# Hybrid decoder, two layers: the pre-norm weight folded into the splitting of the projection weights, and the order of the first tiles and of the layer's end written out

## The chip, the cores and the metric

The kernel runs on one core of a Trainium2 chip. The metric is device time in microseconds (us) of one execution. A core has five engines that each run their own queue of instructions in order: PE (matmul), ACT, DVE and POOL (elementwise work), and SP, which here only issues DMAs.

## The reference

Two layers work on 512 tokens of width 1024. Cut to what matters here:

```python
def rms_norm(x, g):
    return x * lax.rsqrt(mean(x * x, axis=-1) + 1e-6) * g

def hybrid_layer(x, w_in, w_out, g_pre, g_post, ...):
    h = rms_norm(x, g_pre)
    proj = einsum('bsd,de->bse', h, w_in)      # 1024 -> 6400 columns
    ... HGRN2 recurrence (8 heads), sliding-window attention (16 heads), gates ...
    y = einsum('bse,ed->bsd', concat([o_h, o_a]), w_out)   # 2048 -> 1024
    return x + rms_norm(y, g_post)
```

The weight `g_pre` of the first norm scales the columns of `h`, which are the rows of `w_in`: scaling `h` by it or scaling the rows of `w_in` gives the same product.

## The kernel before, in words

**Products in three passes.** Every projection is computed in a reduced float format with both operands split in a high and a low half; `mm3` (L174 to L177) adds stationary high times moving low (or the reverse), low times high, and high times high. So each operand has to be split first. Activations are split when they leave PSUM: `split_psum` (L266 to L268) copies the high half on ACT (`hhi`) and subtracts on DVE (`hlo`). Weights are split by `w_conv`: a piece of 128x512 comes by DMA into one of three `raw` buffers (`w_load`, L152), ACT copies the high half (`whi`, L169), and DVE or POOL subtracts it to get the low half (`wlo`, L170). A raw buffer is free for the next DMA only when the low half of the piece in it is done. There are 264 pieces: per layer 4 for keys and values (`wkv`, two row blocks of 256 columns each), 96 of `w_in` in twelve slabs of eight, and 32 of `w_out`. POOL takes every second piece of `wkv` and of the first slab `QA`, 12 pieces in all; DVE does the other 252.

**Order of the work.** `step()` emits one k step of a projection at a time (three matmuls), then runs what was put off with `later(steps, key, fn)` and is due, then calls `w_conv` so that conversion stays `LEAD` = 4 pieces ahead. `ensure` runs what is still put off when a unit needs its key. Instructions are ordered on each engine by a scheduler that goes by the order in which the program emits them and by its estimate of when their operands are ready; `pin` puts an instruction behind the instruction of the same engine that was emitted just before it. SP issues its DMAs in order too, so a DMA that waits for a buffer holds up those behind it.

**Pre-norm.** `pre_norm` does one tile of 128 tokens: two squares with row sums on ACT (L302, into the one buffer `u`), a sum on DVE (L280), the power -1/2 on POOL (L282), two multiplications by that and by `g_pre` on DVE (L306, `xn`), four transposes on PE for each half (L311), and the split (L267 and L268). Before the first layer it is emitted for all four tiles, ahead of everything else. `g_pre` is read as a row copied to all 128 partitions, two DMAs of 256 KB in each layer (L292).

**End of a layer.** The last output projection (`out` `h1`) runs token tile by token tile. For each half the result is added on DVE (`y`, L732) and squared on ACT (L758); POOL multiplies the first half by `g_post` (L760), DVE the second (L763); then rstd, two fused multiply-adds on DVE (L766) and the DMAs to memory (L767). In layer 0 the next layer's `pre_norm` of the same tile follows at once, and its transposes and splits are put off by `DEFER` = 18 steps. The key and value projection of layer 1 needs them first (`PE pj L175` on `wkv`), then slab `QA`.

## Time and profile before

| | us |
|---|---|
| median of 3 runs (972.87 to 973.04) | 973.0 |
| profiled execution, own time | 975.33 |
| its span | 973.5 |
| PE busy | 921.1 |
| DVE busy | 739.5 |
| ACT busy | 446.6 |
| POOL busy | 289.2 |
| mean granted clock of PE | 0.983 |

The profile is one execution of its own. Its time lies 2.3 us above the median, and 1.8 us of its time lie outside the span. PE is busy for 95% of the span, so the time is that of PE plus the stretches in which PE waits or runs at a lower clock.

### The profile page before, as it was taken

The page shows a single profiled execution, that of the slowest core. Times are in us where ns is not written, and L with a number is a line of the kernel's source. Part 1 is how long each engine was busy: PE and PEld are TensorE (multiplying, and loading weights), DVE is VectorE, ACT ScalarE, POOL GpSimd, SP SyncE. Part 2 cuts the span into 40 slices and gives each one's busy share as a digit, 9 for nine tenths or more (in the row PEclk, how much of TensorE's full clock was granted, in tenths as well). Part 3 has the DMA queues.
Part 4 walks back from the last instruction along what each step waited for, and adds up shares of the span by engine and source line. Part 5 has one row for each costly group of instructions (what it writes and reads, how often), then busy time and mean ns, then how long its engine had stood idle before and what let it go on. Part 6 is the DMA issues. An engine that isn't in the chain of part 4 may idle for free.

```text
span 973.5 us, 18079 instructions
## 1 busy us (share of the span) xinstructions
PE 921.1 (95%) x6716; PEld 754.4 (77%) x6716; DVE 739.5 (76%) x1510; ACT 446.6 (46%) x1071; POOL 289.2 (30%) x314
## 2 busy tenths in 40 slices
...
DMA packets 56711, 101.24 MB, mean 104 GB/s; under 512 B 6448, under 2 KB 9008, under 8 KB 56624
## 3 DMA queue, kind: packets, MB, share of 16 engines
...
q14 instruction: 34, 0.28, 0.1%
HBM read 87.48 MB, written 12.58 MB: 103 GB/s over the span
## 4 chain that ended last, share of the span: by engine, by line
PE 59%; DVE 26%; ACT 5%; issue 4%; DMA 4%; POOL 1%; SPq 0%; DVEq 0%; POOLq 0%; ACTq 0%
PE pj L175 17%; PE pj L177 16%; PE pj L176 16%; DVE wlo L170 6%; DVE a L554 4%; PE sc L428 2%; DMA raw<-in_win_dram 2%; DMA raw<-in_wout_dram 2%; DVE oa L487 1%; PE ac L481 1%; PE sc L596 1%; ACT whi L169 1%; DVE f L528 1%; PE sc L455 1%; ACT s L442 1%
## 5 line engine op out<-in xcount | busy, mean ns | idle before, releaser
L169 ACT CAST whi<-raw 128x512 fp32r<-128x512 f32 x256 | 157.1, 622 | 188.1 <-DMA raw<-in_win_dram 75.9
L170 DVE TENSOR_TENSOR wlo<-raw,whi 128x512 fp32r<-128x512 f32 x248 | 185.7, 763 | 54.1 <-ACT whi L169 52.9
L175 PE MATMUL pj<-hhi,wlo 128*128 128x512 f32 x512 | 207.2, 405 | 2.3 <-DVE wlo L170 2.3
L177 PE MATMUL pj<-hhi,whi 128*128 128x512 f32 x512 | 200.5, 392 | 0.0
L176 PE MATMUL pj<-hlo,whi 128*128 128x512 f32 x512 | 200.3, 391 | 0.0
L175 PEld LDWEIGHTS pj<-hhi,wlo 128*128 128x128 f32 x512 | 96.5, 189 | 23.4 <-DVE wlo L170 4.6
L177 PEld LDWEIGHTS pj<-hhi,whi 128*128 128x128 f32 x512 | 96.4, 188 | 21.2
L176 PEld LDWEIGHTS pj<-hlo,whi 128*128 128x128 f32 x512 | 96.8, 189 | 17.9
L175 PE MATMUL pj<-whi,ops 128*128 128x512 f32 x256 | 104.9, 410 | 4.3 <-ACT q L535 3.5
L175 PE MATMUL pj<-whi,hlo 128*128 128x512 f32 x256 | 102.8, 404 | 0.0
L177 PE MATMUL pj<-whi,ops 128*128 128x512 f32 x256 | 101.4, 396 | 0.0
L176 PE MATMUL pj<-wlo,hhi 128*128 128x512 f32 x256 | 101.4, 396 | 0.0
L177 PE MATMUL pj<-whi,hhi 128*128 128x512 f32 x256 | 101.2, 395 | 0.0
L176 PE MATMUL pj<-wlo,ops 128*128 128x512 f32 x256 | 101.0, 395 | 0.0
L614 POOL TENSOR_TENSOR k<-k,tot 128x256 f32<-128x256 f32 x64 | 51.3, 820 | 83.3 <-PE sc L596 43.5
L175 PEld LDWEIGHTS pj<-whi,ops 128*128 128x128 f32 x256 | 48.9, 191 | 15.9 <-ACT q L535 4.3
L442 ACT ACTIVATE s<-sc,negm 128x128 f32<-128x128 f32 x128 | 45.6, 369 | 27.3 <-DVE negm L436 27.0
L177 PEld LDWEIGHTS pj<-whi,ops 128*128 128x128 f32 x256 | 48.8, 190 | 11.0
L177 PEld LDWEIGHTS pj<-whi,hhi 128*128 128x128 f32 x256 | 48.7, 190 | 10.1
L176 PEld LDWEIGHTS pj<-wlo,ops 128*128 128x128 f32 x256 | 48.8, 191 | 9.3
L449 POOL TENSOR_TENSOR s<-s,sums 128x512 f32<-128x512 f32 x32 | 34.3, 1073 | 71.2 <-DVE sums L447 47.2
L175 PEld LDWEIGHTS pj<-whi,hlo 128*128 128x128 f32 x256 | 48.8, 190 | 8.6
...
## 6 DMA issues: line engine op xcount, KB each, us to landing
raw<-in_win_dram SPq DMA_DIRECT2D x192, 256.0 KB, 2.7
raw<-in_wout_dram SPq DMA_DIRECT2D x64, 256.0 KB, 2.7
...
qs<-stack SPq DMA_DIRECT2D x32, 256.0 KB, 4.7
a<-in_x_dram SPq DMA_DIRECT2D x12, 256.0 KB, 3.1
raw<-in_wkv_dram SPq DMA_DIRECT2D x8, 256.0 KB, 3.9
x_mid<-a SPq DMA_DIRECT2D x8, 256.0 KB, 2.0
a<-x_mid SPq DMA_DIRECT2D x8, 256.0 KB, 3.2
```

Of the source, the lines that this page charges most:

```text
L169: nc.scalar.copy(hi, v)
L170: (nc.gpsimd if i in on_pool and i % 2 else nc.vector).tensor_tensor(lo, v, hi.bitcast(F32), op=ALU.subtract)
L175: nc.tensor.matmul(o, lhsT=sta[1], rhs=mov[0], start=start, stop=False)
L176: nc.tensor.matmul(o, lhsT=sta[0], rhs=mov[1], start=False, stop=False)
L177: nc.tensor.matmul(o, lhsT=sta[0], rhs=mov[0], start=False, stop=stop)
L428: pin(nc.tensor.matmul(S[:, h * 256:(h + 1) * 256], lhsT=q[:, 2 * hp_ + h, t_], rhs=kst[v][p][:, (n - 1) * P:(n + 1) * P], start=(h == 0 a ...
L442: nc.scalar.activation(pt[:, h * P:(h + 1) * P], cur[h], AF.Exp, bias=negm[:, h:h + 1], scale=SCALE, accum_out=sums[:, h:h + 1])
L449: nc.gpsimd.tensor_tensor(pv, pv, sums.unsqueeze(2).broadcast_to([P, 4, P]), op=ALU.mult)
L455: pin(nc.tensor.transpose(T[:, h * P:(h + 1) * P], pt[:, h * P:(h + 1) * P], ident))
L481: pin(nc.tensor.matmul(U, lhsT=vst[v][:, blk, :], rhs=d, start=(i == 0), stop=(i == len(terms) - 1)))
L554: nc.vector.reciprocal(re, e)
L614: nc.gpsimd.tensor_tensor(kv_[:, :, 0, :], kv_[:, :, 0, :], tv[:, :, 1].unsqueeze(2).broadcast_to([P, nb, hh]), op=ALU.mult)
```

## The change

- The factor `g_pre` leaves the pre-norm and goes into the splitting of `w_in` and `wkv`. It comes as one 128x16 tile `gp` (8 KB, one column for each layer and row block). `whi` is now an ACTIVATE with `scale=gp` (L171), `wlo` a fused multiply and subtract on DVE (L174). For a `wkv` piece, which holds two row blocks, each is two instructions of 128x256. Pieces of `w_out` are split as before (L178, L179).
- POOL does no splitting any more; DVE does all pieces.
- `xn` is a plain scaling by the row's rstd: on DVE before the first layer (L320), on ACT between the layers (L319).
- `pre_norm` becomes a class with stages. Before the first layer (`first_norm`) tile 0 goes first, with the four `wkv` pieces pinned around it; then the squares and scalings of tiles 1 and 2; transposes and splits of tiles 1, 2 and 3 (and the squares of tile 3) are put off by 8, 12 and 20 steps. The loads are put in another order: x of tile 0, `ident`, `gp`, the first `wkv` piece, x of tile 1, two pieces, x of tiles 2 and 3, the last piece.
- At the end of a layer the multiplication by `g_post` moves from POOL to DVE (L807, L810), the adds, squares and what follows are pinned, and the next layer's pre-norm of a tile is put off in parts, beside the end of the following tile. `high_priority(200)` on the last adds is gone. `g_post` comes already copied to 128 rows by the host.

Lines of the changed kernel that the text uses: L184 to L186 `mm3`, L289 and L291 rstd, L313 squares, L326 transposes, L328 `hhi`, L335 `hlo`, L778 add of `y`, L807 and L810 times `g_post`, L820 the fused multiply-add.

```diff
-POOL_SLABS = (QA,)
...
-        plan(("in", l, s), [win[l, s, k * P:(k + 1) * P, :] for k in range(KT)])
+        plan(("in", l, s), [win[l, s, k * P:(k + 1) * P, :] for k in range(KT)], [[(l, k)] for k in range(KT)])
...
-    on_pool = set()
-    for key, (first, n) in slab_first.items():
-        if key[0] == "kv" or key[2] in POOL_SLABS:
-            on_pool.update(range(first, first + n))
...
-    def w_conv(n):
+    def w_conv(n, head=False):
...
-            nc.scalar.copy(hi, v)
-            (nc.gpsimd if i in on_pool and i % 2 else nc.vector).tensor_tensor(lo, v, hi.bitcast(F32), op=ALU.subtract)
+            if gains[i]:
+                w = 512 // len(gains[i])
+                for j, (l, k) in enumerate(gains[i]):
+                    c, g = slice(j * w, (j + 1) * w), gp[:, l, k:k + 1]
+                    a = nc.scalar.activation(hi[:, c], v[:, c], AF.Copy, scale=g)
+                    if head:
+                        pin(a)
+                    b = nc.vector.scalar_tensor_tensor(lo[:, c], v[:, c], g, hi[:, c].bitcast(F32), op0=ALU.mult, op1=ALU.subtract)
+                    if head:
+                        pin(b)
+            else:
+                nc.scalar.copy(hi, v)
+                nc.vector.tensor_tensor(lo, v, hi.bitcast(F32), op=ALU.subtract)
...
-        nc.vector.scalar_tensor_tensor(t, ss[:, 0:1], EPS, ss[:, 1:2], op0=ALU.add, op1=ALU.add)
+        pin(nc.vector.scalar_tensor_tensor(t, ss[:, 0:1], EPS, ss[:, 1:2], op0=ALU.add, op1=ALU.add))
         r = sm.tile([P, 1], F32, tag="r1", name="r1")
-        nc.gpsimd.tensor_tensor(r, t, mhalf[:, 0:1], op=ALU.pow)
+        pin(nc.gpsimd.tensor_tensor(r, t, mhalf[:, 0:1], op=ALU.pow))
...
-            nc.sync.dma_start(t[c], g[c * 512:(c + 1) * 512].partition_broadcast(P))
+            nc.sync.dma_start(t[c], g[:, c * 512:(c + 1) * 512])
...
-    def pre_norm(tt, xt, g, hT, key, defer=0):
-        ss = sm.tile([P, 2], F32, tag="ss", name="ss")
-        xn2 = big.tile([P, 2, 512], F32, tag="q", name="xn", bufs=QB)
-        for c in range(2):
-            junk = tmp("u")
-            nc.scalar.activation(junk, xt[c], AF.Square, scale=1.0 / 32.0, accum_out=ss[:, c:c + 1])
-        r = rstd2(ss)
-        for c in range(2):
-            xn = xn2[:, c]
-            nc.vector.scalar_tensor_tensor(xn, xt[c], r, g[c], op0=ALU.mult, op1=ALU.mult)
-            def rest(c=c, xn=xn):
-                o = sc()
+    class PreNorm:
+        def __init__(self, tt, xt, hT, key):
+            self.tt, self.xt, self.hT, self.key = tt, xt, hT, key
+        def squares(self):
+            self.ss = sm.tile([P, 2], F32, tag="ss", name="ss")
+            for c in range(2):
+                pin(nc.scalar.activation(tmp("u"), self.xt[c], AF.Square, scale=1.0 / 32.0, accum_out=self.ss[:, c:c + 1]))
+        def scale(self, on_act):
+            r = rstd2(self.ss)
+            self.xn = big.tile([P, 2, 512], F32, tag="q", name="xn", bufs=QB)
+            for c in range(2):
+                pin(nc.scalar.activation(self.xn[:, c], self.xt[c], AF.Copy, scale=r) if on_act else
+                    nc.vector.tensor_scalar(self.xn[:, c], self.xt[c], r, None, op0=ALU.mult))
+        def turn(self):
+            self.o = [sc(), sc()]
+            for c in range(2):
                 for j in range(4):
-                    pin(nc.tensor.transpose(o[:, j * P:(j + 1) * P], xn[:, j * P:(j + 1) * P], ident))
-                ov = o.rearrange("p (k t) -> p k t", k=4)
-                sl = (slice(None), slice(4 * c, 4 * c + 4), slice(tt * P, (tt + 1) * P))
-                split_psum(hT[0][sl], hT[1][sl], ov)
-            later(defer, key if c == 1 else None, rest)
-            if not defer:
-                run_first()
+                    pin(nc.tensor.transpose(self.o[c][:, j * P:(j + 1) * P], self.xn[:, c, j * P:(j + 1) * P], ident))
+                hi = self.part(0, c)
+                pin(nc.scalar.copy(hi[0], hi[1]))
+        def part(self, which, c):
+            return (self.hT[which][:, 4 * c:4 * c + 4, self.tt * P:(self.tt + 1) * P], self.o[c].rearrange("p (k t) -> p k t", k=4))
+        def low(self, c):
+            lo, src = self.part(1, c)
+            pin(nc.vector.tensor_tensor(lo, src, self.part(0, c)[0].bitcast(F32), op=ALU.subtract))
+            if c:
+                emitted.add(self.key)
+    def first_norm(xts, hT):
+        n = [PreNorm(tt, xts[tt], hT, ("h", 0, tt)) for tt in range(NT)]
+        def split(tt):
+            n[tt].turn()
+            n[tt].low(0)
+            n[tt].low(1)
+        n[0].squares()
+        n[0].scale(False)
+        w_conv(1, True)
+        n[1].squares()
+        split(0)
+        for i in range(2, 5):
+            w_conv(i, True)
+        n[1].scale(False)
+        n[2].squares()
+        n[2].scale(False)
+        later(8, n[1].key, lambda: split(1))
+        def third():
+            n[3].squares()
+            n[3].scale(False)
+            split(2)
+        later(12, n[2].key, third)
+        later(20, n[3].key, lambda: split(3))
...
-                    with tc.high_priority(200 if final else 0):
-                        nc.vector.tensor_tensor(yt[tt][:, ch], o, yt[tt][:, ch], op=ALU.add)
+                    add = nc.vector.tensor_tensor(yt[tt][:, ch], o, yt[tt][:, ch], op=ALU.add)
+                    if final is not None:
+                        pin(add)
...
-                        hT2["gpre"] = load_g(g_pre[l + 1])
...
+            before = norms[-1] if norms else None
+            pin(nc.scalar.activation(tmp("u"), y[:, ch], AF.Square, scale=1.0 / 32.0, accum_out=ss[:, ch:ch + 1]))
             if ch == 0:
-                nc.gpsimd.tensor_tensor(y[:, 0], y[:, 0], hT2["gpost"][0], op=ALU.mult)
+                pin(nc.vector.tensor_tensor(y[:, 0], y[:, 0], hT2["gpost"][0], op=ALU.mult))
                 return
             yg = tmp("s")
-            nc.vector.tensor_tensor(yg, y[:, 1], hT2["gpost"][1], op=ALU.mult)
+            pin(nc.vector.tensor_tensor(yg, y[:, 1], hT2["gpost"][1], op=ALU.mult))
             r = rstd2(ss)
-            for c, v in ((0, y[:, 0]), (1, yg)):
-                nc.vector.scalar_tensor_tensor(xt[c], v, r, xt[c], op0=ALU.mult, op1=ALU.add)
-                nc.sync.dma_start((out if last else x_mid)[tt * P:(tt + 1) * P, c * 512:(c + 1) * 512], xt[c])
-            if not last:
-                pre_norm(tt, xt, hT2["gpre"], hT[l + 1], ("h", l + 1, tt), DEFER)
+            if before:
+                before.scale(True)
+            def rest():
+                if before:
+                    before.turn()
+                    before.low(0)
+                for c, v in ((0, y[:, 0]), (1, yg)):
+                    pin(nc.vector.scalar_tensor_tensor(xt[c], v, r, xt[c], op0=ALU.mult, op1=ALU.add))
+                    nc.sync.dma_start((out if last else x_mid)[tt * P:(tt + 1) * P, c * 512:(c + 1) * 512], xt[c])
+                if before:
+                    before.low(1)
+                if last:
+                    return
+                norms.append(PreNorm(tt, xt, hT[l + 1], ("h", l + 1, tt)))
+                norms[-1].squares()
+                if tt == NT - 1:
+                    norms[-1].scale(True)
+                    def end():
+                        norms[-1].turn()
+                        norms[-1].low(0)
+                        norms[-1].low(1)
+                    later(15, norms[-1].key, end)
+            if before:
+                later(6 if tt == NT - 1 else 3, before.key, rest)
+            else:
+                rest()
...
-    gpre = load_g(g_pre[0])
+    gp = const_tile(g_pre, [P, DEPTH, KT], F32, "gp")
     w_load(1)
-    for tt in range(1, NT):
-        xts.append(x_tile(tt))
-        w_load(1 + tt)
+    xts.append(x_tile(1))
+    w_load(3)
+    xts += [x_tile(2), x_tile(3)]
+    w_load(4)
...
-    for tt in range(NT):
-        pre_norm(tt, xts[tt], gpre, hT[0], ("h", 0, tt))
+    first_norm(xts, hT[0])
...
-    nc.vector.tensor_copy(masks, mraw[:, 0:448])
+    pin(nc.vector.tensor_copy(masks, mraw[:, 0:448]))
...
+    g_pre = np.ascontiguousarray(inp["g_pre"].reshape(DEPTH, KT, 128).transpose(2, 0, 1))
+    g_post = np.ascontiguousarray(np.tile(inp["g_post"][:, None, :], (1, 128, 1)))
```

ACT at the start, before: from the second `hhi` of tile 0 to the first conversion of a `w_in` piece (`hhi` is the split of a pre-norm tile in PSUM buffer `sc`, `u` the squares, `wkv` and `whi` the high halves of weights).

```order
L267 CAST hhi<-sc_80 128x4x128
L302 ACTIVATE u,ss<-x_99 128x512
L267 CAST hhi<-sc_78 128x4x128
L302 ACTIVATE u,ss<-x_104 128x512
L169 CAST wkv<-raw 128x512
L302 ACTIVATE u,ss<-x_104 128x512
L267 CAST hhi<-sc_79 128x4x128
L169 CAST wkv<-raw 128x512
L267 CAST hhi<-sc_80 128x4x128
L267 CAST hhi<-sc_78 128x4x128
L339 COPY s<-pj 128x256
L169 CAST whi<-raw 128x512
```

ACT at the same place now, from the squares of tile 3 (`x_103`) to the second `hhi` of tile 2.

```order
L313 ACTIVATE u,ss<-x_103 128x512
L921 ACTIVATE lb_e<-lb_e 128x16
L171 ACTIVATE whi<-raw,gp 128x512
L399 COPY s<-s 128x2x64
L313 ACTIVATE u,ss<-x_103 128x512
L171 ACTIVATE whi<-raw,gp 128x512 x2
L328 CAST hhi<-sc_78 128x4x128
L328 CAST hhi<-sc_79 128x4x128
L171 ACTIVATE whi<-raw,gp 128x512 x3
L328 CAST hhi<-sc_80 128x4x128
L328 CAST hhi<-sc_78 128x4x128
```

Of the eight `hhi` rows six, those of tiles 0 to 2, stood ahead of the first conversion of a `w_in` piece; now the two of tile 1 stand behind the fifth `whi`, and those of tile 2 behind the eighth.

DVE at the start, before: from the scaling of tile 3 to the second conversion of a `w_in` piece (`xn` is the scaled tile, `hlo` its low half, `wlo` the low half of weights).

```order
L306 SCALAR_TENSOR_TENSOR xn<-x_104,r_200,b 128x512
L268 TENSOR_TENSOR hlo<-sc_78,hhi 128x4x128
L306 SCALAR_TENSOR_TENSOR xn<-x_104,r_200,b 128x512
L826 CAST masks<-u 128x448
L268 TENSOR_TENSOR hlo<-sc_79,hhi 128x4x128
L837 TENSOR_SCALAR nsnk<-snk 128x32
L845 TENSOR_TENSOR lb_mx<-lp 128x8
L170 TENSOR_TENSOR wlo<-raw,whi 128x512
L268 TENSOR_TENSOR hlo<-sc_80,hhi 128x4x128
L848 TENSOR_TENSOR lb_e<-lp,lb_mx 128x8 x2
L170 TENSOR_TENSOR wlo<-raw,whi 128x512
```

DVE now, from the scaling of the first half of tile 3 to the splits of tile 2.

```order
L320 TENSOR_SCALAR xn<-x_103,r_354 128x512
L936 TENSOR_TENSOR lb_c<-lb,lb_b 128x16
L174 SCALAR_TENSOR_TENSOR wlo<-raw,gp,whi 128x512 x2
L335 TENSOR_TENSOR hlo<-sc_78,hhi 128x4x128
L335 TENSOR_TENSOR hlo<-sc_79,hhi 128x4x128
L174 SCALAR_TENSOR_TENSOR wlo<-raw,gp,whi 128x512
L320 TENSOR_SCALAR xn<-x_103,r_354 128x512
L174 SCALAR_TENSOR_TENSOR wlo<-raw,gp,whi 128x512 x2
L335 TENSOR_TENSOR hlo<-sc_80,hhi 128x4x128
L335 TENSOR_TENSOR hlo<-sc_78,hhi 128x4x128
```

Before, one `hlo` of the eight stood behind a `wlo` row. Now three more `wlo` stand ahead of this piece, so `hlo` of tile 1 is behind the fifth and that of tile 2 behind the eighth.

DVE at the end of layer 0, before: from the add of the second half of tile 2 on, with the sums `s` of the rstd (`hlo` is the split of the next layer's tile 0).

```order
L732 TENSOR_TENSOR y<-pj,y 128x512
L280 SCALAR_TENSOR_TENSOR s_5244<-ss 128x1
L763 TENSOR_TENSOR s<-y,b 128x512
L306 SCALAR_TENSOR_TENSOR xn<-a,r_5246,b 128x512 x2
L280 SCALAR_TENSOR_TENSOR s_5289<-ss 128x1
L170 TENSOR_TENSOR wlo<-raw,whi 128x512
L766 SCALAR_TENSOR_TENSOR a<-y,r_5291,a 128x512
L732 TENSOR_TENSOR y<-pj,y 128x512
L766 SCALAR_TENSOR_TENSOR a<-s,r_5291,a 128x512
L268 TENSOR_TENSOR hlo<-sc_80,hhi 128x4x128
L732 TENSOR_TENSOR y<-pj,y 128x512
L280 SCALAR_TENSOR_TENSOR s_5303<-ss 128x1
L268 TENSOR_TENSOR hlo<-sc_78,hhi 128x4x128
```

DVE now, from the add of the second half of tile 1 on.

```order
L778 TENSOR_TENSOR y<-pj,y 128x512
L810 TENSOR_TENSOR s<-y,b 128x512
L289 SCALAR_TENSOR_TENSOR s_5235<-ss 128x1
L289 SCALAR_TENSOR_TENSOR s_5239<-ss 128x1
L335 TENSOR_TENSOR hlo<-sc_80,hhi 128x4x128
L820 SCALAR_TENSOR_TENSOR a<-y,r_5237,a 128x512
L820 SCALAR_TENSOR_TENSOR a<-s,r_5237,a 128x512
L335 TENSOR_TENSOR hlo<-sc_78,hhi 128x4x128
L778 TENSOR_TENSOR y<-pj,y 128x512
L174 SCALAR_TENSOR_TENSOR wlo<-raw,gp,whi 128x512 x2
L807 TENSOR_TENSOR y<-y,b 128x512
```

The two `hlo` of tile 0 stood behind the scaling of tile 1 (`xn`), a conversion and the multiply-adds of tile 2; now they stand beside the multiply-adds of tile 1, and no `xn` is left on DVE.

24 lines of the change are left out of this document (12 added, 12 removed).

## The prediction

> **What bounds the kernel now.** I read the page's first part, then the chain of waits, then the groups by line, and last the timeline at the start, at the layer boundary and at the end. The page and its chain:
>
> ```profile
> PE 921.1 (95%) x6716; PEld 754.4 (77%) x6716; DVE 739.5 (76%) x1510; ACT 446.6 (46%) x1071; POOL 289.2 (30%) x314
> PE 59%; DVE 26%; ACT 5%; issue 4%; DMA 4%; POOL 1%; SPq 0%; DVEq 0%; POOLq 0%; ACTq 0%
> PE pj L175 17%; PE pj L177 16%; PE pj L176 16%; DVE wlo L170 6%; DVE a L554 4%; PE sc L428 2%; DMA raw<-in_win_dram 2%; DMA raw<-in_wout_dram 2%; DVE oa L487 1%; PE ac L481 1%; PE sc L596 1%; ACT whi L169 1%; DVE f L528 1%; PE sc L455 1%; ACT s L442 1%
> ```
>
> PE is the bound, but DVE holds a quarter of the chain, and `wlo` is its largest line. The change adds no matmul and takes none away, so it acts in two ways: on the stretches where PE waits or is slow, and on the price of `whi` and `wlo`. The stretches show in the table of windows (the columns that count are PE busy, DVE busy, and the granted clock, third from the end):
>
> ```profile
> 0.00:10.00 10.00, 7.14 (x12) 2.85 (x12) 1.15 (x5) 3.68 (x7) 1.72 (x7) 1.00 0.71 221
> 10.00:20.00 10.00, 7.26 (x40) 6.62 (x40) 6.83 (x13) 7.36 (x19) 2.32 (x3) 0.66 0.62 199
> 20.00:30.00 10.00, 9.52 (x78) 8.96 (x76) 9.94 (x30) 5.87 (x15) 3.12 (x3) 1.00 0.56 181
> 30.00:40.00 10.00, 9.38 (x50) 8.07 (x51) 9.26 (x37) 5.76 (x19) 3.92 (x3) 1.00 0.41 129
> 490.00:500.00 10.00, 4.60 (x21) 4.60 (x22) 9.44 (x15) 4.98 (x12) 3.90 (x5) 0.66 0.51 158
> ```
>
> The first 30 us and the boundary around 495 are the weak places, both with a clock of 0.66, and DVE is full in one and just after the start of the other.
>
> **The start.** The timeline of PE, ACT and DVE, and the chain's first QA matmul:
>
> ```profile
> 15.11 0.56 PE L175 MATMUL pj<-wkv,hlo 128*128 128x256 f32 x1
> 24.63 1.16 ACT L169 CAST whi<-raw 128x512 fp32r<-128x512 f32 x2
> 27.27 0.68 DVE L268 TENSOR_TENSOR hlo<-sc,hhi 128x512 fp32r<-128x512 f32 x1
> 29.36 0.62 ACT L169 CAST whi<-raw 128x512 fp32r<-128x512 f32 x1 [1.00 <-DMA raw<-in_win_dram]
> 31.41 0.12 PE pj L177
> 31.53 0.23 PE pj L175
> L169 ACT CAST wkv<-raw x2: 602/610/617, 8.9 to 11.0; 128x512 fp32r<-128x512 f32 x2
> raw<-in_win_dram SPq DMA_DIRECT2D x192, 256.0 KB, 2.7
> L152 SPq DMA_DIRECT2D raw<-in_wkv_dram x4: 379/411/727, 3.1 to 10.3; - x4
> DMA to landing us min/median/max: 4.9/5.6/6.4
> ```
>
> The last row is the time of the four `wkv` DMAs of the row above it. The first piece is there at 8.9 us, behind two `g_pre` DMAs of 256 KB, the last at 10.3 + 4.9 = 15.2. The first key and value matmul runs at 15.11, the last `hlo` is done at 27.95, and slab QA starts at 31.53, after the last key and value matmuls (31.41). From there PE hardly waits (9.38 busy of the window from 30 to 40, and the rest lies ahead of 31.4), so the start is worth exactly what that 31.53 becomes.
>
> Two things shorten it. Without 512 KB in front the pieces come sooner: at the 221 GB/s of the first window that is 2.4 us, with half and one and a half times that as ends; since the loads of `x` are also put in another order, I take 3.0 for the last piece, 12.2. And tile 0 goes first, with nothing of tiles 1 to 3 ahead of it, so its first matmul comes at about 11, some 4 us sooner. One thing lengthens it, and it ends last: `hhi` of tile 1 stands behind five `whi`, and those need five raw buffers of which there are three. The DMAs of the fourth and fifth `w_in` piece go out only when the first and second `wlo` are done, and each takes 2.7 us. With 0.6 to 0.7 us for each `whi`, `wlo`, `hhi`, `hlo` and square: tile 0 is projected by 16.6; then its copy and two `whi`, and the two `wlo` by 19.4; the masks and the squares of tile 3 meanwhile; pieces four and five land at 21.4 and 22.1, their `whi` end at 23.0 and 23.7, `hhi` of tile 1 at 24.2 and 24.7, and `hlo`, behind the fifth `wlo`, at 26.1 and 26.7. PE has nothing to do from 16.6 to 26. Tile 2 waits in the same way for `whi` six to eight and has its `hlo` at 30.8, tile 3 at 34.2, and QA starts at 35.5. With the last `wkv` piece 0.9 us sooner or 1.6 us later it is 35.5 or 36.7, so the start of the DMAs decides little: the ring of three does. That is +4.0; a part of the instructions that I put in a row may overlap, so I take +4, range +0.5 to +6.
>
> **The price of the pieces.** By line, then the rows that are nearest to the new forms (for a source line: min, median and max in ns):
>
> ```profile
> L170 DVE TENSOR_TENSOR wlo<-raw,whi x248: 616/686/1776, 26.7 to 945.0; 128x512 fp32r<-128x512 f32 x124
> L170 POOL TENSOR_TENSOR wlo<-raw,whi x8: 1259/1298/1396, 25.3 to 507.5; 128x512 fp32r<-128x512 f32 x8
> L716 DVE SCALAR_TENSOR_TENSOR ops<-sc,gh,ops x16: 736/746/751, 399.4 to 950.1; 128x512 fp32r<-128x512 f32 x16
> L306 DVE SCALAR_TENSOR_TENSOR xn<-a,r,b x12: 737/744/1807, 10.2 to 505.6; 128x512 f32<-128x512 f32 x12
> L169 ACT CAST whi<-raw x256: 603/621/657, 23.5 to 944.4; 128x512 fp32r<-128x512 f32 x128
> L302 ACT ACTIVATE u<-a x12: 626/630/636, 3.6 to 503.1; 128x512 f32<-128x512 f32 x12
> L715 ACT ACTIVATE ops<-sc,gh x16: 682/687/691, 398.7 to 949.4; 128x512 fp32r<-128x512 f32 x16
> L526 ACT ACTIVATE f<-pj 128x512 f32<-128x512 f32 x16 | 9.6, 600 | 12.0 <-PE pj L177 11.9
> ```
>
> `wlo` with a scalar column takes 0.745 where the plain subtraction takes 0.686: +0.06 on 192 pieces, 11.5 us of DVE time. What of it ends last is read from the chain: 6% of 973.5 is 58 us of `wlo`, about three quarters of them (192 of 256) pieces of `w_in`, so 44 us, at 0.06 in 0.686 is +3.8. The chain counts what released what, and a piece that comes 0.06 late is at times caught by the lead of four pieces: 0 if all of them are, 3.8 if none is; since DVE is full just where the chain runs through it, I take +3. `whi` becomes an ACTIVATE with a column as scale. From SBUF with a plain number it takes 0.630 against 0.621, and from PSUM with a column 0.687 against 0.600 with a number (L526): +0.01 to +0.09 on a piece. `whi` is 1% of the chain, 10 us or 16 pieces: +0.2 to +1.4; I take +0.7, midway, since the column is the nearer likeness. Together +3.7, range 0 to +5.5.
>
> The Trainium skill, in "ScalarE: Activation LUTs", section "What ACT_TABLE_LOAD costs", states that each pointer operand adds about 93 ns to an ACTIVATE; the pair L715 and L526 here differs by 87 ns, so the trace agrees from PSUM, and no row shows it from SBUF. By the page alone the term would be 16 pieces by 0.093, an estimate of +1.5 in place of +0.7.
>
> The 12 pieces that leave POOL cost DVE 12 by 0.69, 8 us. POOL's passes were not free for DVE:
>
> ```profile
> 491.68 1.26 POOL L170 TENSOR_TENSOR wlo<-raw,whi 128x512 fp32r<-128x512 f32 x1
> 491.75 1.74 DVE L766 SCALAR_TENSOR_TENSOR a<-y,r,a 128x512 f32<-128x512 f32 x1 [0.43 <-POOL r L282]
> ```
>
> The same form takes 0.74 where nothing holds it (L716, L306), so a pass of POOL held it for 1.0 us. If all 12 did, DVE gains 12 and loses 8, if none, it loses 8. All lie in the two places costed on their own, so I book nothing for them here. The skill's "Perfetto Trace Analysis", section "Optimizing Scalar/DVE Operations", says that POOL and DVE share a read port, so that moving work between them might not help; the trace agrees with the 1.0 us.
>
> **The layer boundary.** The timeline there:
>
> ```profile
> 479.90 2.47 DVE L306 SCALAR_TENSOR_TENSOR xn<-a,r,b 128x512 f32<-128x512 f32 x2
> 488.19 1.05 ACT L267 CAST hhi<-sc 128x512 fp32r<-128x512 f32 x2
> 489.31 0.39 PE L177 MATMUL pj<-whi,ops 128*128 128x512 f32 x1
> 494.67 0.68 DVE L268 TENSOR_TENSOR hlo<-sc,hhi 128x512 fp32r<-128x512 f32 x1
> 495.40 0.58 PE L175 MATMUL pj<-wkv,hlo 128*128 128x256 f32 x1 [5.70 <-DVE hlo L268]
> 512.28 0.39 PE L175 MATMUL pj<-hhi,wlo 128*128 128x512 f32 x1
> ```
>
> `hhi` of tile 0 is done at 489.2, but its `hlo` stands behind other DVE work until 494.67, so PE waits 5.7 us and runs the next two clock windows at half speed. Now that `hlo` comes right behind its `hhi`: the 5.7 go. But the last `wlo` and `hlo` that QA needs are those of tile 3, and their chain is add, square, rstd, multiply-add, square, rstd, scale, transpose, split for each tile, now with the scaling on ACT behind that tile's rstd and all of it pinned in one row. `xn` of tile 0 moves from 479.9 to about 482.7 (PE stands still for 1.8 us in the middle of h1); that of tile 1 comes at about 493, and that of tile 2, whose rstd stands behind the multiplication and the squares of tile 3, at about 502.9. PE then waits from about 500 to 503.5, and QA starts at about 513.1 to 514.2 instead of 512.28. I take +1.3. The ends: -6, if the whole wait and the clock come back (5.7, with the half-speed windows as margin), and +4, if tile 3 also comes late by an ACT pass and the 2.7 us of a DMA.
>
> **The end.** The last tile:
>
> ```profile
> 965.52 0.63 ACT L758 ACTIVATE u<-y 128x512 f32<-128x512 f32 x1 [3.06 <-DVE y L732]
> 965.71 0.69 DVE L732 TENSOR_TENSOR y<-pj,y 128x512 f32<-128x512 f32 x1 [0.28 <-PE pj L177]
> 966.32 1.26 POOL L760 TENSOR_TENSOR y<-y,b 128x512 f32<-128x512 f32 x1 [2.94 <-ACT u L758]
> 966.44 1.70 DVE L763 TENSOR_TENSOR s<-y,b 128x512 f32<-128x512 f32 x1
> 968.06 0.15 DVE L280 SCALAR_TENSOR_TENSOR s<-ss 128x1 f32<-128x1 f32 x1
> ```
>
> On DVE the multiplication of the first half waits for its square, as POOL's did until 966.32, and stands ahead of the last add: that ends at 967.5 instead of 966.4, its square at 968.3, and the sum of the squares runs at 968.4 instead of 968.06. The second multiplication loses its 1.0 us of stall, but no longer ends last. +0.4, range 0.2 to 0.6.
>
> **The sum.** +4.0 +3.7 +1.3 +0.4 = +9.4 on the profiled execution's 975.3 (a span of 973.5 and 1.8 around it), 984.7. That execution lies 2.3 above the median of the runs, 973.0, on which it is 982.4.
>
> **The rivals.**
>
> - The start and the boundary win what they were rearranged for. For it speak the row at 15.11 (first matmul 4 us sooner, and if tile 1 follows without the five `whi`, QA starts that much sooner) and the 5.7 us at 495.40. Against it speaks the order on ACT and DVE, which has no way round for `hhi` of tile 1. It decides if QA of layer 0 starts before 31.5 less the price of the pieces. Time: -4 -5.7 +3.7 +0.4, or 967.4.
> - The pieces' price is hidden and only start, boundary and end count: 973.0 +4.0 +1.3 +0.4 = 978.7. For it speaks that DVE is busy for only 76%; against it the 6% of `wlo` on the chain.
> - One gain, one loss: the boundary gives back what the start loses (-4 +4), and pieces and end are partly hidden: 973 to 975.
> - The new idle 10 us of PE at the start cost a second time: the two windows with 0.66 above come with idle stretches of PE, and the 72 key and value matmuls of tiles 1 to 3, 0.12 each in the row at 31.41, take that once more at half speed, up to 8.6, of which a half or so is hidden by the waits: 986.7. The skill's "TensorE: Matmul & The Clock Gate", Part 1, describes such a gate, which lowers the clock after an idle window.
>
> **How the numbers follow.** Chances: the forecast 0.45, pieces hidden 0.17, clock 0.10, one gain one loss 0.12, the wins 0.16. The likeliest is 982.4, with its own range of 977 to 987. To leave out no more than 2 in 10, the range reaches down over the case of one gain and one loss and part of the wins: 969 to 987. A measurement of this kernel can tell about 0.2%, 1.9 us. Faster by more: the wins and a little of the mixed case, 0.19. Within: most of the mixed case, 0.10. Slower: 0.71.
>
> **What would show it.** Right: first `wkv` matmul near 11, then a wait of PE of some 9 us for `hlo` of tile 1, and QA at about 35.5. The median of `wlo` on `w_in` at 0.745, of `whi` at 0.63 to 0.71. No 5.7 us wait at the boundary, but shorter ones for `xn` and `hlo`, and QA of layer 1 some 1.3 us later, counted from the end of h1's matmuls. Wrong: `hlo` of tile 1 ahead of 20 us, or the wait of QA of layer 1 gone with nothing in its place.

## The result and the profile after

The changed kernel takes 990.36 us (median of 4 runs, 989.63 to 992.93), the kernel before 972.93 on the same chip: 1.0183 times as long, 95% interval 1.0166 to 1.0199. The direction was forecast (982.4, slower with a chance of 0.71), but the time lies 8.0 us above the forecast and 3.4 above the end of its range, 987. The profiled execution of the changed kernel took 989.63, its span is 987.9, 14.4 more than before.

The page: busy times of the engines, and the chain by engine.

```profile
PE 920.6 (93%) x6716; PEld 752.0 (76%) x6716; DVE 739.6 (75%) x1530; ACT 471.0 (48%) x1087; POOL 259.1 (26%) x294
PE 46%; DVE 28%; issue 7%; ACT 6%; DMA 3%; POOL 2%; DVEq 0%; POOLq 0%; ACTq 0%
```

PE does the same work (920.6 us busy, 921.1 before), and it holds 46% of the chain instead of 59%. DVE is no busier than before. So the 14.4 us are places where PE waits, and what the clock does after them. To find the places, the start of the n-th of the 3,264 projection matmuls is set against the start of the same one in the profile of before (counted on the two traces; the numbers are a kernel's own time less before's, in us; "1600" is in h1 of layer 0, "1850" in slab QA of layer 1):

```
n of the matmul      110    200    260    400   1600   1850   1910   3263  end of span
where              in QA  in QA  2nd slab      end of   in QA  2nd slab  last
                   of l.0       passed        layer 0  of l.1   passed
after               +5.9   +5.9  +12.4  +13.3   +7.2   +9.9  +16.3  +13.0  +14.4
```

Five steps make it up: the start +5.9, the second slab of layer 0 +6.5 (+5.9 to +12.4), the layer boundary +2.7, the second slab of layer 1 +6.4, the end +1.4: +22.9. The stretches between them give back 8.5. In those the profile of before shows five windows of 3.4 us in which PE is granted half its clock (from 107, 128, 220, 367 and 735 us on), and that of after shows none outside its steps. Inside each of the five the delay of after shrinks by 1.4 to 1.7 us, some 7.8 together. Two rows of before show such windows (PE busy, PEld, DVE, ACT, POOL, granted clock, DMA share, GB/s):

```profile
220.00:230.00 10.00, 10.00 (x109) 7.77 (x110) 7.37 (x15) 4.42 (x14) 3.02 (x4) 0.83 0.31 99
730.00:740.00 10.00, 8.18 (x30) 6.23 (x29) 8.23 (x17) 3.32 (x7) 4.74 (x5) 0.83 0.46 130
```

**The start.** PE's timeline, then two windows (same columns):

```profile
10.72 0.39 PE L184 MATMUL pj<-wkv,hlo 128*128 128x256 f32 x1 [0.96 <-DVE hlo L335]
...
25.61 0.58 PE L184 MATMUL pj<-wkv,hlo 128*128 128x256 f32 x1 [8.32 <-DVE hlo L335]
...
28.33 1.54 PE L326 MATMUL sc<-ident,xn 128*128 128x128 f32 x8
...
37.23 0.40 PE L184 MATMUL pj<-hhi,wlo 128*128 128x512 f32 x1
```

```profile
10.00:20.00 10.00, 5.07 (x32) 4.12 (x32) 7.63 (x23) 6.12 (x17) 1.09 (x2) 0.96 0.71 230
20.00:30.00 10.00, 4.39 (x23) 4.39 (x24) 8.31 (x30) 6.99 (x16) 0.54 (x1) 0.53 0.62 185
```

The first row stood at 15.11 before. Then PE waits 8.32 us for `hlo` of tile 1, which stands behind the fifth `whi` and `wlo`. The clock goes to half at 19.1, 1.8 us into this wait, and stays there for 10.2 us, until 29.35. So matmuls that come every 0.12 us in this projection come every 0.21 at first (25.99, 26.20, 26.41). QA starts at 37.23 instead of 31.36, 5.9 later, and so are the matmuls behind it. (The forecast took 31.53 from the chain; the timeline of before has QA's first matmul at 31.36.)

**The second slab.** ACT from 60 us on, then the next matmul of PE:

```profile
60.19 1.40 ACT L171 ACTIVATE whi<-raw,gp 128x512 fp32r<-128x512 f32 x2 [2.36 <-DMA raw<-in_win_dram]
64.55 0.72 ACT L171 ACTIVATE whi<-raw,gp 128x512 fp32r<-128x512 f32 x1 [2.96 <-DMA raw<-in_win_dram]
68.06 0.62 ACT L438 CAST rot<-rot 128x512 fp32r<-128x512 f32 x1 [2.78 <-POOL rot L435]
69.28 0.62 ACT L438 CAST rot<-rot 128x512 fp32r<-128x512 f32 x1 [0.60 <-POOL rot L436]
69.80 1.33 ACT L171 ACTIVATE whi<-raw,gp 128x512 fp32r<-128x512 f32 x2
```

```profile
71.36 0.79 PE L184 MATMUL pj<-hhi,wlo 128*128 128x512 f32 x1 [3.51 <-DVE wlo L174]
```

And ACT of the kernel before, at the same work:

```profile
57.57 0.62 ACT L169 CAST whi<-raw 128x512 fp32r<-128x512 f32 x1 [2.11 <-DMA raw<-in_win_dram]
58.41 0.62 ACT L169 CAST whi<-raw 128x512 fp32r<-128x512 f32 x1 [0.21 <-DMA raw<-in_win_dram]
59.26 0.62 ACT L169 CAST whi<-raw 128x512 fp32r<-128x512 f32 x1 [0.24 <-DMA raw<-in_win_dram]
61.29 0.62 ACT L391 CAST rot<-rot 128x512 fp32r<-128x512 f32 x1 [1.41 <-POOL rot L388]
64.19 0.62 ACT L391 CAST rot<-rot 128x512 fp32r<-128x512 f32 x1 [2.28 <-POOL rot L389]
```

`rot` is QA's rotation, which waits for POOL. Before, all pieces of the second slab were converted ahead of its last two casts; now two `whi` stand behind them, and ACT idles 2.78 us for POOL with the next weights behind. PE waits 3.51 us for that `wlo`, and the clock is at half from 70.3 to 77.1, of which 5.8 us lie behind the wait (0.83 over these 20 us, 1.00 at the same place before):

```profile
60.00:80.00 20.00, 16.49 (x61) 13.01 (x60) 7.79 (x11) 4.59 (x7) 2.50 (x2) 0.83 0.70 189
550.00:570.00 20.00, 16.39 (x62) 12.98 (x61) 9.38 (x13) 4.65 (x9) 5.07 (x4) 0.83 0.40 116
```

The second row is the same place in layer 1. Nothing in the diff names this place: the scheduler set another order there.

**The price of the pieces** (min, median and max in ns):

```profile
L171 ACT ACTIVATE whi<-raw,gp x192: 705/724/759, 15.9 to 932.7; 128x512 fp32r<-128x512 f32 x192
L174 DVE SCALAR_TENSOR_TENSOR wlo<-raw,gp,whi x192: 643/746/1572, 18.1 to 934.5; 128x512 fp32r<-128x512 f32 x192
```

**The boundary**, PE:

```profile
490.77 0.66 PE L326 MATMUL sc<-ident,xn 128*128 128x128 f32 x4 [1.82 <-ACT xn L319]
...
501.53 0.65 PE L326 MATMUL sc<-ident,xn 128*128 128x128 f32 x4 [0.50 <-ACT xn L319]
...
511.53 1.97 PE L326 MATMUL sc<-ident,xn 128*128 128x128 f32 x8 [3.77 <-ACT xn L319]
```

The wait of 5.70 is gone, but three waits for `xn` on ACT take its place, and the clock is at half for 6.8 us around the end of the last of them (510.6 to 517.5). All waits of PE for `xn` between the layers after, and all for `hlo` there before (us in total, times, longest):

```profile
PE sc L326 <- ACT xn L319: 6.1, 3, 3.8
PE pj L175 <- DVE hlo L268: 6.7, 2, 5.7
```

After, 1.9 us of waits for `hlo` come on top, so PE waits 8.0 us here where it waited 6.7.

**The end**, after PE's last matmul at 978.3:

```profile
978.45 0.74 DVE L820 SCALAR_TENSOR_TENSOR a<-s,r,a 128x512 f32<-128x512 f32 x1
979.12 0.68 DVE L778 TENSOR_TENSOR y<-pj,y 128x512 f32<-128x512 f32 x1
979.89 0.63 ACT L805 ACTIVATE u<-y 128x512 f32<-128x512 f32 x1 [2.95 <-DVE y L778]
980.64 0.69 DVE L807 TENSOR_TENSOR y<-y,b 128x512 f32<-128x512 f32 x1 [0.85 <-ACT u L805]
981.25 0.68 DVE L778 TENSOR_TENSOR y<-pj,y 128x512 f32<-128x512 f32 x1
982.79 0.16 DVE L289 SCALAR_TENSOR_TENSOR s<-ss 128x1 f32<-128x1 f32 x1
```

The first add of the last tile is pinned behind the multiply-adds of tile 2, and the second add behind the multiplication that waits for a square.

### The profile page after: what moved, and what is told of

The parts are those of the page before. It is cut to its first block, busy times and chain, and to the rows that moved or that the text cites. A ratio compares the mean times of both kernels' runs of the same rounds, so it can differ in the third digit from the quotient of the medians.

```text
span 987.9 us, 18086 instructions
## 1 busy us (share of the span) xinstructions
PE 920.6 (93%) x6716; PEld 752.0 (76%) x6716; DVE 739.6 (75%) x1530; ACT 471.0 (48%) x1087; POOL 259.1 (26%) x294
## 4 chain that ended last, share of the span: by engine, by line
PE 46%; DVE 28%; issue 7%; ACT 6%; DMA 3%; POOL 2%; DVEq 0%; POOLq 0%; ACTq 0%
PE pj L184 13%; PE pj L186 12%; PE pj L185 12%; DVE wlo L174 5%; DVE a L601 5%; DMA raw<-in_win_dram 2%; PE sc L475 2%; DVE oa L534 1%; DMA raw<-in_wout_dram 1%; PE sc L643 1%; ACT whi L171 1%; PE ac L528 1%; ACT s L489 1%; DVE f L575 1%; DVE wlo L179 1%
## 5 line engine op out<-in xcount | busy, mean ns | idle before, releaser
L184 PE MATMUL pj<-hhi,wlo 128*128 128x512 f32 x512 | 209.4, 409 | 11.0 <-DVE wlo L174 10.8
L186 PE MATMUL pj<-hhi,whi 128*128 128x512 f32 x512 | 202.1, 395 | 0.0
L171 ACT ACTIVATE whi<-raw,gp 128x512 fp32r<-128x512 f32 x192 | 135.9, 723 | 121.9 <-DMA raw<-in_win_dram 75.7
L174 DVE SCALAR_TENSOR_TENSOR wlo<-raw,gp,whi 128x512 fp32r<-128x512 f32 x192 | 150.9, 803 | 40.1 <-ACT whi L171 39.3
L184 PEld LDWEIGHTS pj<-hhi,wlo 128*128 128x128 f32 x512 | 97.5, 190 | 34.3 <-DVE wlo L174 15.2
L186 PEld LDWEIGHTS pj<-hhi,whi 128*128 128x128 f32 x512 | 97.3, 190 | 21.5
L184 PE MATMUL pj<-whi,ops 128*128 128x512 f32 x256 | 103.5, 404 | 3.2 <-ACT q L582 3.2
L184 PE MATMUL pj<-whi,hlo 128*128 128x512 f32 x256 | 102.3, 402 | 2.2 <-ACT whi L171 2.2
L186 PE MATMUL pj<-whi,hhi 128*128 128x512 f32 x256 | 100.5, 393 | 0.0
L186 PE MATMUL pj<-whi,ops 128*128 128x512 f32 x256 | 100.2, 392 | 0.0
L178 ACT CAST whi<-raw 128x512 fp32r<-128x512 f32 x64 | 39.6, 621 | 63.8 <-DMA raw<-in_wout_dram 29.6
L184 PEld LDWEIGHTS pj<-whi,ops 128*128 128x128 f32 x256 | 48.2, 188 | 13.4 <-ACT q L582 4.0
L184 PEld LDWEIGHTS pj<-whi,hlo 128*128 128x128 f32 x256 | 48.0, 188 | 11.3 <-ACT whi L171 3.0
L179 DVE TENSOR_TENSOR wlo<-raw,whi 128x512 fp32r<-128x512 f32 x64 | 44.9, 710 | 15.4 <-ACT whi L178 15.2
L186 PEld LDWEIGHTS pj<-whi,ops 128*128 128x128 f32 x256 | 48.0, 188 | 10.7
L185 PEld LDWEIGHTS pj<-wlo,hhi 128*128 128x128 f32 x256 | 48.2, 188 | 10.4 <-DVE wlo L174 2.3
L186 PEld LDWEIGHTS pj<-whi,hhi 128*128 128x128 f32 x256 | 48.1, 188 | 9.8
```

Source lines behind the costliest of these rows:

```text
L171: a = nc.scalar.activation(hi[:, c], v[:, c], AF.Copy, scale=g)
L174: b = nc.vector.scalar_tensor_tensor(lo[:, c], v[:, c], g, hi[:, c].bitcast(F32), op0=ALU.mult, op1=ALU.subtract)
L178: nc.scalar.copy(hi, v)
L179: nc.vector.tensor_tensor(lo, v, hi.bitcast(F32), op=ALU.subtract)
L184: nc.tensor.matmul(o, lhsT=sta[1], rhs=mov[0], start=start, stop=False)
L185: nc.tensor.matmul(o, lhsT=sta[0], rhs=mov[1], start=False, stop=False)
```

## The experiments

In each heading stand the median, and the ratio to the kernel before on the same chip with its 95% interval. The kernel before has medians of 972.9 to 973.5 beside these runs, so a difference of medians between two headings carries some 0.5 us from that. A step is read on one profiled execution each.

### Splits of tiles 1 to 3 at once: 982.24 us, 1.0093 (1.0061 to 1.0124)

On the changed kernel:

```diff
-        later(8, n[1].key, lambda: split(1))
+        split(1)
...
-        later(12, n[2].key, third)
-        later(20, n[3].key, lambda: split(3))
+        third()
+        split(3)
```

> The changed kernel with one edit: the transposes and splits of tiles 1 to 3 and the squares of tile 3 are emitted at once instead of after 8, 12 and 20 steps, so hhi and hlo stand ahead of most conversions of w_in. Theory (the order holds tile 1 back): the 8.3 us wait of PE for hlo of tile 1 is gone, slab QA starts at 26 to 31 instead of 37.2, and the kernel is 6 to 10 us faster than the changed one, about 980 to 984. Rival (the late raw buffers hold the start back in any order): QA still starts at 35 to 37 and the time stays at 989 to 991.

QA starts at 28.91 and its later matmuls are 1.9 us earlier than before, not 5.9 later: 7.8 by this edit, and the medians differ by 8.1. No wait of 8 us is left; all waits of PE for `hlo` in the program:

```profile
PE pj L184 <- DVE hlo L335: 3.0, 5, 1.0
```

So the delay of the splits behind the conversions is the loss of the start, and without it the start is a gain. The steps at the second slabs (+3.7 and +5.3) and at the boundary (+4.3) are still there.

### The old order at the second slab, by a pin: 981.79 us, 1.0087 (1.0061 to 1.0114)

On the changed kernel; conversion may not run past the second slab while QA is worked on, and QA's last casts on ACT and DVE are pinned:

```diff
-        w_conv(ahead.get(u.key, first + n) + ... + LEAD)
+        goal = ahead.get(u.key, first + n) + ... + LEAD
+        w_conv(min(goal, first + 2 * KT) if u.key[0] == "in" and u.key[2] == QA else goal)
...
-                    nc.scalar.copy(h.bitcast(F32R), r)
-                    nc.vector.tensor_tensor(r.bitcast(F32R), r, h, op=ALU.subtract)
+                    keep = pin if s == 0 and m == 3 else (lambda ins: ins)
+                    keep(nc.scalar.copy(h.bitcast(F32R), r))
+                    keep(nc.vector.tensor_tensor(r.bitcast(F32R), r, h, op=ALU.subtract))
```

> The changed kernel with one edit: in slab QA the last pair of rotary results is pinned on ACT and DVE behind the conversions of the second slab, and conversion doesn't run past that slab before QA ends, so that eight whi stand ahead of the casts of rot as in the kernel before (six in the changed one). Theory (the 6.5 us that the second slab loses in each layer come from that order): the waits of PE for wlo fall from 12 us to under 4, the two steps of 6.5 shrink to 0 to 3, and the kernel is 5 to 10 us faster, less than 2 times 6.5 because part of a delay there was given back later in the layer. Rival (the longer forms themselves keep the pieces late): the steps stay above 5 and the time at 988 to 991.

The steps at the second slabs are +0.6 and +1.2 in place of +6.5 and +6.4. So an order on ACT and DVE is the cause, not the longer instructions as such. The median gains only 8.6 of these 11, and the pin put the casts late: ACT reaches them at 77.15 to 80.8 us, and attention waits later on, as PE's longest wait between 70 and 130 us shows (at matmul 340 the delay is 16.4, at 400 again 9.3):

```profile
PE sc L477 <- ACT s L491: 4.8, 2, 4.1
```

### `whi` plain, the factor in `wlo` alone: 978.99 us, 1.0067 (1.0041 to 1.0093)

On the changed kernel. The high half is of the unscaled weight here, so the two halves do not add up exactly to the product.

```diff
-                    a = nc.scalar.activation(hi[:, c], v[:, c], AF.Copy, scale=g)
+                    a = nc.scalar.copy(hi[:, c], v[:, c])
```

> The changed kernel with one edit: the high half of a w_in and wkv piece is the plain copy of before without the factor, the low half stays the fused form (so the split is less exact). The built order of the second slab is then again eight whi ahead of rot. Order theory: as the run with the pinned slab, 5 to 10 us faster. Price theory (0.1 us for each whi with a column as scale, 192 of them, 17 or so on the chain): 1.5 to 2 us faster, with the steps at the second slab still above 5.

The start stays at +5.9, the boundary at +2.8, and both steps at the second slabs are 0.0. The median falls by 11.4 us, nearly the 12.9 of those two steps.

### `wlo` plain: 972.17 us, 0.9995 (0.9970 to 1.0019)

On the changed kernel. The low half lacks the factor here.

```diff
-                    b = nc.vector.scalar_tensor_tensor(lo[:, c], v[:, c], g, hi[:, c].bitcast(F32), op0=ALU.mult, op1=ALU.subtract)
+                    b = nc.vector.tensor_tensor(lo[:, c], v[:, c], hi[:, c].bitcast(F32), op=ALU.subtract)
```

> The changed kernel with one edit: the low half of a w_in and wkv piece is the plain subtraction of before, so the factor is left out of the product; the high half keeps the ACTIVATE with a column as scale (0.72 us). The built order of the second slab is again that of before. Order theory: as with the plain high half, the two steps at the second slab are 0 to 2, the time 977 to 982. Price theory (what the plain high half won was the 0.1 us of each whi): the steps stay above 4, the time at 986 to 990.

The steps at the second slabs are 0.0 here too, with `whi` still long. So one longer form alone leaves the order as it was; it takes both to change it. The time came out below what was expected. On ACT the order of this run differs from that of the changed kernel by the places of 10 of 1,087 instructions: the casts of `rot` at the two second slabs, and single `whi` and `u` in the attention of each layer. Against the run with plain `whi`, the medians differ by 6.8 us. It isn't shown that this is the price of the longer `wlo` alone: the two runs have the same order at the second slabs, but ACT's orders part from 124 us on in the attention of layer 0, and again in layer 1.

### The layer's end as before: 983.09 us, 1.0105 (1.0075 to 1.0134)

On the changed kernel, the `final` and `pre_norm` of before between the layers and at the end (POOL multiplies by `g_post`, nothing pinned, `xn` on DVE), without the factor:

```diff
-                before.scale(True)
-                ...
-                later(6 if tt == NT - 1 else 3, before.key, rest)
+                nc.gpsimd.tensor_tensor(y[:, 0], y[:, 0], hT2["gpost"][0], op=ALU.mult)
...
+                pre_norm(tt, xt, hT2["gpre"], hT[l + 1], ("h", l + 1, tt), DEFER)
```

> The changed kernel with one edit: the end of the layer and the pre-norm between the layers as in the kernel before (y times g_post on POOL, nothing pinned, xn on DVE, splits put off by 18 steps), the factor still in the weights. Theory (the new end costs by itself): the step at the boundary goes from +2.7 to about 0 and the tail from +1.4 to 0, 3 to 5 us faster, 985 to 987. Rival (the new end is neutral, the boundary's loss comes from the longer conversions of layer 1's first pieces): under 1.5 us faster.

Between matmuls 1600 and 1850 it gains 1.9 where the new end loses 2.7, and from the last matmul to the end of the span it gains 0.4 where the new one loses 1.4: 6.4 us, against 7.3 in the medians, more than the 3 to 5 that were expected. PE's waits at the boundary:

```profile
499.82 0.39 PE L184 MATMUL pj<-wkv,hlo 128*128 128x256 f32 x1 [1.85 <-DVE hlo L277]
506.69 0.66 PE L382 MATMUL sc<-ident,xn 128*128 128x128 f32 x4 [2.19 <-DVE xn L377]
508.35 0.58 PE L184 MATMUL pj<-wkv,hlo 128*128 128x256 f32 x1 [1.01 <-DVE hlo L277]
```

The 5.70 us wait of before is not there either: with `g_pre` and POOL's pieces out of the way, the old order needs 1.85 there. The new order was not needed to remove it.

### The factor alone, in the old order: 973.48 us, 0.9998 (0.9974 to 1.0022)

On the kernel before: `gp` in place of `g_pre`, both longer forms, every piece on DVE, `xn` a plain scaling; nothing else is moved.

```diff
-            nc.scalar.copy(hi, v)
-            (nc.gpsimd if i in on_pool and i % 2 else nc.vector).tensor_tensor(lo, v, hi.bitcast(F32), op=ALU.subtract)
+                    nc.scalar.activation(hi[:, c], v[:, c], AF.Copy, scale=g)
+                    nc.vector.scalar_tensor_tensor(lo[:, c], v[:, c], g, hi[:, c].bitcast(F32), op0=ALU.mult, op1=ALU.subtract)
...
-            nc.vector.scalar_tensor_tensor(xn, xt[c], r, g[c], op0=ALU.mult, op1=ALU.mult)
+            nc.vector.tensor_scalar(xn, xt[c], r, None, op0=ALU.mult)
```

> The kernel before with one edit: the factor in the weights (both new forms, all on DVE, xn a plain scaling, gp loaded in place of g_pre), first tiles and layer end as before. Order theory: the second slab loses 6 to 7 us in each layer as in the changed kernel, the start gains 2 to 3 (no g_pre loads), the time is 7 to 12 us above the kernel before, 980 to 986. Rival (the second slab's loss needs the new start or the new end): 971 to 977.

Below what was expected, for a reason that was not in it: the start gains 5.9 us (QA at 25.50), and PE is busy without a gap where the changed kernel idles:

```profile
20.00:30.00 10.00, 10.00 (x73) 9.43 (x72) 9.48 (x47) 7.00 (x21) 0.00 (x0) 1.00 0.51 158
```

The second slab costs it +5.2 in layer 0, and there PE waits for the same `wlo` (between 55 and 95 us):

```profile
PE pj L184 <- DVE wlo L176: 3.3, 1, 3.3
```

In layer 1 it costs +5.4, and +4.2 up to matmul 2000. So the step at the second slab comes with the two forms alone, without any of the changes of order. The time falls into the range of the rival (971 to 977), but not on its ground, that the slab's loss needs the new start or the new end. In the profiles the gains at the start (5.9), at the boundary (1.1) and in the stretches without a step stand against 14.8 lost at the slabs and behind them; in the medians nothing is left. Against the run with the old end, which differs from this one mainly in the start, QA starts 12.6 us sooner (-5.9 against +6.7).

### Before, nothing on POOL: 968.47 us, 0.9954 (0.9928 to 0.9979)

```diff
-POOL_SLABS = (QA,)
+POOL_SLABS = ()
...
-        if key[0] == "kv" or key[2] in POOL_SLABS:
+        if False:
```

> The kernel before with one edit: no splitting on POOL, plain forms. My booking of nothing: within 2 us of the kernel before, 971 to 976, the stalls of DVE beside POOL gone and 12 more pieces on it. Rival (DVE is full at the start and the boundary and pays for every piece): 4 to 8 us slower.

Twelve instructions moved, 4.5 us, outside what was expected on either side. In the profiles the start gains 2.5 and the boundary 1.1. There the multiply-add that took 1.74 beside POOL is short, and the wait of 5.70 becomes 2.67 and 1.88 (DVE, then PE):

```profile
492.89 0.75 DVE L766 SCALAR_TENSOR_TENSOR a<-y,r,a 128x512 f32<-128x512 f32 x1
```

```profile
484.29 0.58 PE L175 MATMUL pj<-wkv,hlo 128*128 128x256 f32 x1 [2.67 <-DVE hlo L268]
492.83 0.39 PE L175 MATMUL pj<-wkv,hlo 128*128 128x256 f32 x1 [1.88 <-DVE hlo L268]
```

### The changed kernel mended: 970.28 us, 0.9974 (0.9953 to 0.9995)

The changed kernel with the splits at once, the old end (diffs above), and a limit and a pin at the second slab in a narrower form than in the run with the pin alone:

```diff
+        if u.key == qa or (u.key == ("in", u.key[1], QA + 1) and slab_done[qa] < slab_steps[qa]):
+            goal = min(goal, slab_first[qa][0] + 2 * KT - (slab_done[qa] < slab_steps[qa]))
+        w_conv(goal)
...
+                    keep = pin if s == 0 and m == 3 else (lambda ins: ins)
+                    keep(nc.scalar.copy(h.bitcast(F32R), r))
```

> The changed kernel with three edits: splits of tiles 1 to 3 at once, layer end as before, and the last rotary casts of slab QA pinned behind the conversions of the second slab, which are traced no further before QA ends. If the three losses add (start 7.8, second slab 6.5 in each layer less what is given back, boundary and tail 4): 963 to 972, faster than both. If the pins only move the wait into the attention: 974 to 980.

The three mends take 20.1 us off the changed kernel, and the result is 0.3% below before, with an interval that ends just under 1. The second slab of layer 0 costs +1.4, and 3.1 more follow up to matmul 340.

### The factor alone, with the casts pinned: 966.09 us, 0.9923 (0.9898 to 0.9949)

On the run with the factor alone, with the pin of the diff before this one (against the run with the pin alone, the limit is one piece lower until QA is done, and only QA's last casts on ACT are pinned, not the subtractions on DVE):

```diff
-                    nc.scalar.copy(h.bitcast(F32R), r)
+                    keep = pin if s == 0 and m == 3 else (lambda ins: ins)
+                    keep(nc.scalar.copy(h.bitcast(F32R), r))
```

> The kernel before with the factor in the weights (as the run with the fold alone, 973.5) and the last rotary casts of slab QA pinned behind the second slab's conversions: both longer forms kept, only the order changed. Order theory: the step of 5 us at the second slab falls to under 2 in both layers, the time to 966 to 970. Price theory: the steps stay at 4 to 5 and the time at 972 to 975.

The instructions are the same and the edit names only the two second slabs; 7.4 us less than without the pins. (Behind these places the built order changes too, in the attention of both layers.) The step of 5.2 is 1.3, and of PE's waits for `wlo` between 55 and 95 us, 0.8 and 0.5 are left:

```profile
PE pj L184 <- DVE wlo L176: 0.8, 1, 0.8
PE pj L185 <- DVE wlo L176: 0.5, 2, 0.3
```

3.5 us are lost a little later, in the third slab. This is the fastest version that computes the whole product: 0.8% below before, 24 us below the change.

### The factor alone, `whi` plain: 962.89 us, 0.9897 (0.9861 to 0.9934)

On the run with the factor alone; the halves again do not add up exactly.

```diff
-                    nc.scalar.activation(hi[:, c], v[:, c], AF.Copy, scale=g)
+                    nc.scalar.copy(hi[:, c], v[:, c])
```

> The kernel before with the factor in the low half only: plain copy for the high half, fused form for the low half (the split is less exact), which gives the second slab its old order without a pin and whi its old 0.62. Start as in the fold alone (QA 5.9 sooner), no step at the second slab: 9 to 11 us below the fold alone, 962 to 966. If the 0.06 of each wlo shows: 967 to 970.

No step at any slab of either layer, and 10.6 us less than with the longer `whi`. It shows what the fold brings when the high half stays short and the order holds, and is not a version to use.

### The factor in the split of the activations: 970.62 us, 0.9981 (0.9955 to 1.0007)

On the run with nothing on POOL; weights are split as before, and the transposed tile is scaled when it leaves PSUM, where the factor is one column for 128 rows:

```diff
-                split_psum(hT[0][sl], hT[1][sl], ov)
+                for j in range(4):
+                    k, tk = 4 * c + j, slice(tt * P, (tt + 1) * P)
+                    hi, lo, col = hT[0][:, k, tk], hT[1][:, k, tk], gp[:, g, k:k + 1]
+                    nc.scalar.activation(hi, ov[:, j], AF.Copy, scale=col)
+                    nc.vector.scalar_tensor_tensor(lo, ov[:, j], col, hi.bitcast(F32), op0=ALU.mult, op1=ALU.subtract)
```

> The kernel before with nothing on POOL and the factor moved to the split of the pre-norm (four ACT and four DVE passes of 128x128 with a column of gp for each half tile instead of one each of 128x512); pieces plain. Against the run without POOL (968.5) it saves the g_pre loads (2 to 3 us at the start) and pays 16 times 0.5 us on ACT and DVE at the two places where DVE is full: 966 to 972. Faster than 966 if the loads were all that held the start back, slower than 972 if the split's passes end last there.

Not told apart from before, and no better than the run it is built on (968.47). The pieces stay short and no slab shows a step, but four small instructions for each split come into the chain of the pre-norm. The boundary loses 2.4 us where the run without POOL gains 1.1, and its first wait, 2.67 us without this edit, is

```profile
486.69 0.57 PE L175 MATMUL pj<-wkv,hlo 128*128 128x256 f32 x1 [3.57 <-DVE hlo L317]
```

### Matmuls put into the gap at the start: 988.06 us, 1.0148 (1.0109 to 1.0187)

On the changed kernel; the product of zeros is used nowhere.

```diff
             n[tt].turn()
+            if tt == 1:
+                for _ in range(6):
+                    pin(nc.tensor.matmul(warm, lhsT=zero[:, 0:P], rhs=zero, start=True, stop=True))
```

> The changed kernel with one edit: six matmuls on a tile of zeros (1.2 us each, their result unused) stand on PE between the transposes of tile 1 and its key and value projection, in the 8.3 us in which PE waits. If the half clock of 10.2 us behind that wait comes from the wait: the granted clock stays at 1.0 there, the projection of tile 1 starts at the same 25.6 and runs at 0.12 instead of 0.21 a matmul, and slab QA starts 1.5 to 2 us sooner, at 35.2 to 35.7. If the clock goes by something else: still half at 19 to 29, QA at 37.2 or later.

The clock stays at 1.00 where it was 0.53:

```profile
20.00:30.00 10.00, 6.79 (x39) 4.74 (x37) 9.18 (x34) 7.48 (x16) 0.54 (x1) 1.00 0.63 189
...
25.98 0.38 PE L184 MATMUL pj<-wkv,hlo 128*128 128x256 f32 x1 [3.18 <-DVE hlo L335]
...
36.41 0.40 PE L184 MATMUL pj<-hhi,wlo 128*128 128x512 f32 x1
```

The zeros take PE from 17.48 to 22.80, and the 3.18 us of waiting that are left bring no half clock. Tile 1's projection runs at full speed, but it starts 0.4 us later than in the changed kernel. From there to QA it takes 10.43 us in place of 11.62, so QA is only 0.8 us sooner, where 1.5 to 2 were expected. The median is 2.3 below that of the changed kernel, but the intervals of the two ratios overlap. So the half clock goes with the empty stretch, but only 1.2 us of the start's 5.9 are owed to it.

## Why the prediction missed, step by step

Its sum in profile terms was 975.3 + 9.4 = 984.7; the profiled execution took 989.63. That is 4.9 of the miss. The other 3.0 are the basis: the execution it was summed on lies 2.3 above its median, that of the changed kernel 0.7 below its own.

| term | forecast | measured |
|---|---|---|
| start | +4.0 | +5.9 |
| price of the pieces, spread | +3.7 | +4.4 (second slabs +12.9, between the steps -8.5) |
| boundary | +1.3 | +2.7 |
| end | +0.4 | +1.4 |
| 12 pieces off POOL | 0 | -4.5 by themselves |

**The start: right in mechanism, low in size.** First matmul forecast "near 11", seen at 10.72; a wait "of some 9 us" for `hlo` of tile 1, seen as 8.32; QA at 35.5, seen at 37.23. The +5.9 is just inside the term's own range. The half clock was kept as a rival of 4.3 us more and left out of the sum; it came (0.53), but with it gone QA is only 0.8 us sooner. The rest of the 1.9 was not separated. That the splits' delay is the cause is shown by the run with the splits at once (7.8 us).

**The pieces: right price, wrong place.** `wlo` has its 0.746. `whi` has 0.724, +0.10 to the plain cast, against +0.01 to +0.09 by the rows from which it was bounded. The Trainium skill, "ScalarE: Activation LUTs", section "What ACT_TABLE_LOAD costs", states about 93 ns for each pointer operand; this row, from SBUF, agrees with it (0.094 over the 0.630 of the squares, which have a number as scale). What failed is the step "pieces" itself: it assumed that the longer instructions stand in the same order and spread +3.7 over the chain. Instead both together made the scheduler place two conversions behind a cast that waits for POOL, +6.5 in each layer. That it takes both forms is shown by the two runs with one of them each (0.0 at both slabs), that the fold suffices by the run with the factor alone, and that the order and not the price makes most of it by the pin (5.2 to 1.3). That the total nevertheless came near +3.7 is chance: the profile of before has five windows of half clock between the steps, in which some 7.8 us of the delay come back, and that of after has none. Whether other executions share that is not shown. What the longer forms cost where the order holds was not measured apart; the forecast's +3 for `wlo` is neither confirmed nor refuted.

**The boundary: right in mechanism, half in size.** The 5.70 us wait went and waits for `xn` came in its place, 1.82 (1.8 was forecast) and 3.77 (3.5). PE waits 1.3 us more there than before, which is what was forecast. The other 1.4 were not told apart: the half clock that the forecast gave no price here lasts 6.8 us in both profiles, but 5.9 of it lie behind the wait now (511.53 to 517.5) and 4.6 did before (495.40 to 500.0). The forecast also took it for granted that the old order keeps its wait; with the factor out of it that order does better by 4.6 us.

**The end: too low by 1.0.** The forecast had the second add wait for a multiplication. It missed that the first add, too, is pinned behind two multiply-adds of tile 2 (979.12, 0.8 us after PE's last matmul starts).

**POOL: wrong.** "I book nothing": DVE loses 8 and gains up to 12 by its own numbers. The run without POOL shows -4.5 us in the medians; in its profile 2.5 lie at the start and 1.1 at the boundary, where DVE is full. The Trainium skill, "Perfetto Trace Analysis", section "Optimizing Scalar/DVE Operations", says that moving work between the two might not help; here it did, by 4.5 us. The changed kernel takes the same pieces off POOL; what that brings it was not measured apart.

**The range** ended at 987 because every term that could go wrong upward was taken alone. Start, order at the slabs, boundary and end all came out above their terms together, and for the order at the slabs there was no term.
